# FFN heads of a decoder trunk: weight sums and gate splits put behind the norm, a seven-operation reciprocal root, one raw quarter in the norm's buffer, other tile addresses

## The chip, the cores and the metric

The kernel runs on one core of a Trainium2 chip, in one launch. The metric is the time of an execution on the device in microseconds (us): the median of several runs. The profile and the trace come from one more, profiled execution. Engines are called TensorE (PE in the rows; PEld is its weight load), VectorE (DVE), ScalarE (ACT), GpSimd (POOL) and SyncE (SP, which issues most of the DMAs).

## The reference

The kernel computes a small decoder trunk in fp32 on 512 tokens of 1024 features: two layers of FFN, mixer, FFN. The mixer is a gated convolution in the first layer and sparse attention in the second. Each of the six sub-layers has a norm with a scale, a shift and a gate from a conditioning vector.

```
def adaln(x, g, shift, scale):
    return rms_norm(x, g) * (1 + scale[:, None, :]) + shift[:, None, :]

def swiglu(h, w_in, w_out):
    g, u = jnp.split(h @ w_in, 2, axis=-1)
    return (jax.nn.silu(g) * u) @ w_out
...
        h = adaln(x, norm_g[i, 0], shift[:, 0], scl[:, 0])
        x = x + HALF * gate[:, 0, None, :] * swiglu(h, ffn_w_in[i, 0], ffn_w_out[i, 0])
        h = adaln(x, norm_g[i, 1], shift[:, 1], scl[:, 1])
...
        x = x + gate[:, 1, None, :] * y
        h = adaln(x, norm_g[i, 2], shift[:, 2], scl[:, 2])
        x = x + HALF * gate[:, 2, None, :] * swiglu(h, ffn_w_in[i, 1], ffn_w_out[i, 1])
```

The FFNs are 2816 wide. They are numbered f=0 to 3 here, in the order in which they run.

## The kernel before

`x` lies transposed in SBUF, eight tiles of 128 features by 512 tokens. Every fp32 matrix product is done as three products of fp32r parts (`mm3`, L178 to L180): a value is split into a high part (a copy by ScalarE, L174) and a low part (a subtraction by VectorE, L175), and high by high, low by high and high by low are summed. The names end in `hi`/`lo` or `h`/`l` accordingly. "A group of three" below is one `mm3`.

A sub-layer ends with a tail (`ty`) that works in two halves of 256 tokens, so that the next norm can begin with half 0 while half 1 is still in the tail. The residual (L344) updates `x`, ScalarE squares it (`sq`), and the squares are summed in `nacc` (L243). `Norm.finish` then, for each half, sums over the features on TensorE (`pr`, L260), takes `nv` on VectorE, then the reciprocal root in eleven small operations on 128x2 values (`rs_i` to `rs_r`, L206 to L214), makes two diagonal tiles (`dg`, L267) and spreads them over the partitions with a matmul (`pr`, L268). `piece` makes the normed activation for each of eight feature tiles: `hfull` (L317, VectorE), `hhi` (L319, ScalarE), `hlo` (L320, VectorE). The first matmuls on it are `hs` in `head_start`.

FFNs f=1 to 3 compute most of their columns by a scheme with seven products of half-size blocks in place of eight. Its activation blocks (`th`, `tl`) are made in `quarters`; its weight blocks in `seven_products(j)` come from four raw quarters of a weight tile: two sums of quarters made by DMAs (`qa`), two made by adds (`qb`, L509 and L510), one raw quarter (`a`, named `a22` in the code, L506) and the tile `wraw`. For the first j of each such FFN the two adds run on GpSimd, later on VectorE. `p` (L536) is a copy of the first product that must be made before the accumulator is written again. Ahead of these stands one more pair of columns (`gu`), whose gate weights are `wh` and `wl`.

The engines' queues are in program order, as a scheduler fixed them when the program was built; `tc.high_priority()` moves work forward in them, and `issue_after` (used by the change) keeps an instruction behind another. Tiles live in pools; a tile with a tag takes over the buffer of the tile with that tag before it and waits for its last reader. `tmp` tiles rotate over four buffers of 512 columns. `shift` is a small unused tile that moves everything behind it in the pool to another address.

Of the kernel before, what the change touches and what calls it, by code (L numbers as in the profile page):

```python
# [4 lines left out]

# [17 lines left out]
P = 128  # L23
D = 1024
T = 512
HT = T // 2
KD = D // P
# [26 lines left out]
def decoder_kernel(ctx, tc, xT, cT, ng, adaw, adab, ffi, ffo, cwi, cw, cwo,  # L54
# [8 lines left out]
    def shift(p, n):  # L63
        p.tile([P, n // 4], F32, name="shift")

    shift(pool(ctx, "edge", 1, side="right"), 32)
    cst = pool(ctx, "cst", 1)
    wp = pool(ctx, "wp", 4)
    tp = pool(ctx, "tp", 1)
# [18 lines left out]

    ada_es = ctx.enter_context(ExitStack())
    ap = ada_es.enter_context(tc.tile_pool(name="ada", bufs=4))  # L90
    cond = ap.tile([P, D], F32, name="cond", bufs=1)
    x = [cst.tile([P, T], F32, name=f"x{d}") for d in range(KD)]
    ngs = cst.tile([P, NSUB * KD], F32, name="ngs")
# [107 lines left out]
    def rsqrt(v, n):  # L201
        def small(name, dt=F32):
            return sp.tile([P, n], dt, name=name, padded_shape=[P, 16], bufs=2)

        i = small("rs_i", I32)
        nc.vector.tensor_scalar(i, v.bitcast(I32), 1, None, op0=ALU.logical_shift_right)  # L206
        j = small("rs_j", I32)
        nc.vector.tensor_scalar(j, i, -1.0, RSQ, op0=ALU.mult, op1=ALU.add)
        r = j.bitcast(F32)
        for it in range(3):  # L210
            a, b, q = small("rs_a"), small("rs_b"), small(f"rs_r{it}")
            nc.vector.scalar_tensor_tensor(a, r, -0.5, r, op0=ALU.mult, op1=ALU.mult)
            nc.vector.tensor_mul(b, a, v)
            nc.vector.scalar_tensor_tensor(q, b, 1.5, r, op0=ALU.add, op1=ALU.mult)  # L214
            r = q
        return r

# [8 lines left out]
    class Norm:  # L228
        def __init__(self, s):
            self.s = s  # L230
            self.acc = tp.tile([P, T], F32, name="nacc", tag="nacc", bufs=1)
            self.n = [0, 0]
            self.pr = []

        def square(self, d, a, b, late):
            first = self.n[a // HT] == 0
            if first:
                nc.scalar.activation(self.acc[:, a:b], x[d][:, a:b], AF.Square)
            else:
# [12 lines left out]

        def finish(self, hfs):
            with tc.high_priority():
                n = 2 * len(hfs)
                self.pr += [psum("pr", "pr") for _ in hfs]
                pv = self.pr[hfs[0]]
                for t in range(n):
                    c = hfs[0] * HT + t * P
                    nc.tensor.matmul(pv[:, HT + t:HT + t + 1], self.acc[:, c:c + P], ones[:, 0:1], start=True, stop=True)  # L260
                v = sp.tile([P, n], F32, name="nv", tag="nv", padded_shape=[P, NB])
                nc.vector.tensor_scalar(v, pv[:, HT:HT + n], 1.0 / D, EPS, op0=ALU.mult, op1=ALU.add)
                r = rsqrt(v, n)
                for i, hf in enumerate(hfs):
                    dg = tmp("dg", HT, "dg").rearrange("p (a b) -> p a b", a=2)
                    for t in range(2):
                        nc.vector.tensor_scalar(dg[:, t, :], ident, r[:, 2 * i + t:2 * i + t + 1], None, op0=ALU.mult)  # L267
                    nc.tensor.matmul(self.pr[hf][:, 0:HT], ones, dg.rearrange("p a b -> p (a b)"), start=True, stop=True)  # L268


        def start(self):
            pv = self.all = psum("pr", "pr")
            with tc.high_priority():
                for d in range(KD):
                    dst = self.acc if d == 0 else tmp("sq", tag="sq")
                    nc.scalar.activation(dst, x[d], AF.Square)
                    if d:
                        nc.vector.tensor_tensor(self.acc, self.acc, dst, ALU.add)
                for t in range(NB):
                    nc.tensor.matmul(pv[:, t:t + 1], self.acc[:, t * P:(t + 1) * P], ones[:, 0:1], start=True, stop=True)  # L280
                v = sp.tile([P, NB], F32, name="nv", tag="nv", padded_shape=[P, NB])
                nc.vector.tensor_scalar(v, pv[:, 0:NB], 1.0 / D, EPS, op0=ALU.mult, op1=ALU.add)
                r = rsqrt(v, NB)
                dg = tmp("dg").rearrange("p (a b) -> p a b", a=NB)
                for hf in range(2):
                    for t in range(2 * hf, 2 * hf + 2):
                        nc.vector.tensor_scalar(dg[:, t, :], ident, r[:, t:t + 1], None, op0=ALU.mult)
                    nc.tensor.matmul(self.all[:, hf * HT:(hf + 1) * HT], ones,
                                     dg[:, 2 * hf:2 * hf + 2].rearrange("p a b -> p (a b)"), start=True, stop=True)
# [23 lines left out]
        def piece(self, d, hf):  # L313
            a, b = HALVES[hf]
            sc, sh = mod(self.s, 0, d), mod(self.s, 1, d)
            xr = tmp("xr", HT, "xr") if self.full is None else self.full[:, d, a:b]
            nc.vector.scalar_tensor_tensor(xr, x[d][:, a:b], sc, self.pr[hf][:, 0:HT], op0=ALU.mult, op1=ALU.mult)  # L317
            hi = self.hi[d][:, a:b]
            nc.scalar.activation(hi, xr, AF.Identity, bias=sh)  # L319
            nc.vector.scalar_tensor_tensor(self.lo[d][:, a:b], xr, sh, hi, op0=ALU.add, op1=ALU.subtract)  # L320

        def quarters(self, tt):
            self.th, self.tl = [[tt.tile([P, KD // 2, HT], F32R, name=f"t{e}{j}", tag=f"t{e}{j}") for j in range(4)] for e in "hl"]
# [25 lines left out]

    def head_start(nrm, h, jobs):
        os = [psum("hs") for _ in jobs]
        for hf, (a, b) in enumerate(HALVES):
            with tc.high_priority():
                for d in range(KD):
                    nrm.piece(d, hf)
            m = KD - 3 * hf
            order = [(n, k) for k in range(m) for n in range(len(jobs))]
            order += [(n, k) for n in range(len(jobs)) for k in range(m, KD)]  # L360
            for n, k in order:
                w, wc, kw = jobs[n](k)
                project(os[n][:, a:b], w, wc, h, [(kw, k)], k == 0, k == KD - 1, a, b)
        return os
# [66 lines left out]
    def ffn_first(s, f, nrm, nxt, extra, ahead, first, soon, own):  # L431
        with ExitStack() as es:
            hp = pool(es, "hp", 1)
            hid = Hidden(es, 18)
            h = nrm.alloc(hp)
            nj = FIRST
# [37 lines left out]
    def ffn(s, f, nrm, nxt, w0, ahead):  # L474
        with ExitStack() as es:
# [7 lines left out]
            def seven_products(j):  # L483
# [3 lines left out]
                whi = wp.tile([P, 2, QT], F32R, name="whi", tag="whi", bufs=3)  # L487
                wlo = wp.tile([P, 2, QT], F32R, name="wlo", tag="wlo", bufs=3)
                qa = next(sums)()
                a22 = tmp("a22")  # L490
                qb = swa.tile([P, 2, QT], F32, name="qb")
                ah_, al_ = (sw.tile([P, 2, QT], F32R, name=f"qa{e}", bufs=2) for e in "hl")
                bh_, bl_ = (sw.tile([P, 3, QT], F32R, name=f"qb{e}") for e in "hl")
# [11 lines left out]
                nc.sync.dma_start(raw.rearrange("p a b -> p (a b)"), ffi[f, j, 0].rearrange("p k n -> p (k n)"))  # L505
                nc.sync.dma_start(a22, quart(1, 1))  # L506

                eng = nc.gpsimd if j == nj else nc.vector
                eng.tensor_tensor(qb[:, 0], halves[1], raw[:, 0], ALU.add)  # L509
                eng.tensor_tensor(qb[:, 1], qb[:, 0], raw[:, 1], ALU.add)  # L510
                split(raw, whi, wlo)
                if qa is halves:
                    for n, q in enumerate(qa):
# [35 lines left out]
                keep(e[:, 0:2].rearrange("p a b -> p (a b)"))  # L549

            js = [(j, c) for j in range(nj) for c in range(2)]
            tt = pool(es, "tt", 1, side="right")
            swa = pool(es, "swa", 1, side="right")
            with ExitStack() as tf_es:
                nrm.alloc_seven(hp, pool(tf_es, "tf", 1))
                h = nrm.hi, nrm.lo
                with ExitStack() as hw_es:
                    hw = pool(hw_es, "hw", 1)
                    shift(hw, 64)
                    w = w0 + [weights(ffi[f, j, c], KD, P, hw, 1, wp) for j, c in js[len(w0):]]  # L560

                    gate = weights(ffi[f, nj, 0], KD, P, to=[tt.tile([P, D], F32R, name="w" + e, tag=f"t{e}1") for e in "hl"])
                    os = head_start(nrm, h, [(lambda k, w=w_: (w, 0, k)) for w_ in w])
                os += pair(f, nj, h, gate=gate)
                nrm.quarters(tt)
            nj += 1
# [58 lines left out]
    def conv(s, nrm, nxt, extra, w0, ahead, own):  # L625
        with ExitStack() as es:
            h_es = es.enter_context(ExitStack())
            hp = pool(h_es, "hp", 1)
            ca = pool(es, "cva", 2, side="right")
            h = nrm.alloc(hp)  # L630
            ks = [(k, k) for k in range(KD)]
# [701 lines left out]
```

## Time and profile before

| | |
|---|---|
| median of 3 runs | 1986.33 us (1984.27 to 1987.23) |
| the profiled execution | 1991.76 us, span 1990.0 us |
| TensorE busy | 1935.0 us (97%), 12648 matmuls |
| VectorE busy | 1497.1 us (75%) |
| ScalarE busy | 876.3 us (44%) |
| GpSimd busy | 211.1 us (11%) |
| mean granted TensorE clock | 0.991 of full |
| chain that ended last | TensorE 75%, VectorE 12%, DMA 7%, ScalarE 3% |

The span is the part of the profiled execution that the trace covers. Busy time says how long an engine had an instruction under way; matmuls overlap each other, so the pace of TensorE is read from starts, not from durations. The clock is what was granted to TensorE, as a share of 2.4 GHz.

### The profile page before, as it was taken

The numbers are of one execution on the slowest core, as the hardware profiler recorded it, in microseconds if no ns is written. First come the engines' busy times: TensorE is split into PE (matmuls) and PEld (weight loads), VectorE is DVE, ScalarE is ACT, GpSimd is POOL, SyncE is SP. The second block draws the span as 40 slices with busy tenths as digits, with TensorE's granted clock in tenths as the row PEclk, the third lists the DMA queues.
The fourth block names the chain that finished last, engine by engine and source line by source line (L and its number), as shares of the span: only waits on it lengthen the run. The fifth ranks groups of instructions, "written<-read, shape, count | busy, mean of one in ns | idle before, by whom it ended". The sixth has DMA issues, their size and how long they took to land.

```text
span 1990.0 us, 32476 instructions
## 1 busy us (share of the span) xinstructions
PE 1935.0 (97%) x12648; PEld 1747.0 (88%) x12648; DVE 1497.1 (75%) x2594; ACT 876.3 (44%) x1414; POOL 211.1 (11%) x287
## 2 busy tenths in 40 slices
PE   6999999999999999999999999999989899999999
PEld 4878888898899899999989999999878788898989
DVE  8878888674468686778868677885887878686865
ACT  3422222242235343444534344455777765343532
POOL 0000000100020000001000000001354431000000
PEclk9999999999999999999999999999999899999999
DMA  8888999432246465534646553143211123665622
GB/s 315 293 316 315 325 319 327 161 106 85 85 125 183 132 162 157 149 106 117 181 129 164 153 153 107 45 150 96 54 53 49 60 64 108 184 175 149 170 69 75
DMA packets 113111, 306.88 MB, mean 154 GB/s; under 512 B 13947, under 2 KB 14219, under 8 KB 112956
## 3 DMA queue, kind: packets, MB, share of 16 engines
q1 hardware_dynamic: 97308, 274.81, 41.0%
q0 software_dynamic: 15648, 29.99, 8.8%
q8 instruction: 99, 1.62, 0.3%
q14 instruction: 56, 0.46, 0.1%
HBM read 301.60 MB, written 3.15 MB: 153 GB/s over the span
## 4 chain that ended last, share of the span: by engine, by line
PE 75%; DVE 12%; DMA 7%; ACT 3%; issue 2%; SPq 0%; POOL 0%; DVEq 0%; ACTq 0%; POOLq 0%
PE gu L178 10%; PE gu L180 10%; PE gu L179 10%; PE y L178 6%; PE y L179 6%; PE y L180 6%; DMA adaraw<-in_adaw 6%; DVE wlo L175 3%; PE hs L178 2%; PE hs L179 2%; DVE adaraw L129 2%; PE hs L180 2%; PE cv L179 2%; PE cv L178 2%; PE cv L180 2%
## 5 line engine op out<-in xcount | busy, mean ns | idle before, releaser
L174 ACT ACTIVATE whi<-wraw 128x1024 fp32r<-128x1024 f32 (+2 forms) x283 | 282.0, 1001 | 508.4 <-PE y L179 251.9
L175 DVE TENSOR_TENSOR wlo<-wraw,whi 128x1024 fp32r<-128x1024 f32 (+2 forms) x283 | 326.6, 1155 | 60.5 <-ACT whi L174 58.5
L179 PE MATMUL gu<-hlo,whi 128*128 128x256 f32 (+1 forms) x808 | 258.4, 320 | 0.0
L178 PE MATMUL gu<-hhi,whi 128*128 128x256 f32 (+1 forms) x808 | 258.1, 319 | 0.0
L180 PE MATMUL gu<-hhi,wlo 128*128 128x256 f32 (+1 forms) x808 | 257.4, 319 | 0.0
L178 PE MATMUL y<-ahi,whi 128*128 128x512 f32 x587 | 230.4, 395 | 0.9 <-ACT ahi L174 0.9
L179 PE MATMUL y<-alo,whi 128*128 128x512 f32 x587 | 229.8, 394 | 0.4 <-DVE alo L175 0.4
L180 PE MATMUL y<-ahi,wlo 128*128 128x512 f32 x587 | 229.3, 393 | 0.0
L129 DVE CUSTOM_DVE_ANT_0 adaraw<-adaraw,cond 128x1024 f32<-128x1024 f32 x144 | 174.6, 1224 | 38.5 <-DMA adaraw<-in_adaw 36.8
L178 PEld LDWEIGHTS gu<-hhi,whi 128*128 128x128 f32 x808 | 151.7, 188 | 13.0
L180 PEld LDWEIGHTS gu<-hhi,wlo 128*128 128x128 f32 x808 | 151.7, 188 | 12.3
L179 PEld LDWEIGHTS gu<-hlo,whi 128*128 128x128 f32 x808 | 151.7, 188 | 12.0
L503 POOL DMA_DIRECT2D qa<-in_ffi x54 | 64.9, 1202 | 756.5 <-DMA qa<-in_ffi 289.1
L178 PEld LDWEIGHTS y<-ahi,whi 128*128 128x128 f32 x587 | 109.9, 188 | 29.2 <-ACT ahi L174 5.2
L179 PEld LDWEIGHTS y<-alo,whi 128*128 128x128 f32 x587 | 110.7, 189 | 26.6 <-DVE alo L175 2.9
L180 PEld LDWEIGHTS y<-ahi,wlo 128*128 128x128 f32 x587 | 110.8, 189 | 23.9
L587 DVE SCALAR_TENSOR_TENSOR x<-y,mods,x 128x512 f32<-128x512 f32 x72 | 54.0, 750 | 102.1 <-PE y L180 101.6
L178 PE MATMUL gu<-th,qbh 128*128 128x256 f32 x456 | 126.9, 279 | 2.6 <-ACT qbh L174 2.6
L180 PE MATMUL gu<-th,qbl 128*128 128x256 f32 x456 | 126.5, 279 | 1.8 <-DVE qbl L175 1.8
L178 PE MATMUL gu<-th,qah 128*128 128x256 f32 x456 | 126.1, 277 | 0.6 <-ACT p L536 0.6
L179 PE MATMUL gu<-tl,qbh 128*128 128x256 f32 x456 | 126.7, 278 | 0.0
L179 PE MATMUL gu<-tl,qah 128*128 128x256 f32 x456 | 126.0, 276 | 0.0
(308 smaller groups left out, 5232.4 us busy)
## 6 DMA issues: line engine op xcount, KB each, us to landing
adaraw<-in_adaw SPq DMA_DIRECT2D x144, 512.0 KB, 6.1
wraw<-in_ffi SPq DMA_DIRECT2D x119, 512.0 KB, 3.9
qa<-in_ffi SPq DMA_DIRECT2D x114, 256.0 KB, 3.7
qa<-in_ffi POOLq DMA_DIRECT2D x54, 512.0 KB, 6.4
wraw<-in_ffo SPq DMA_DIRECT2D x72, 384.0 KB, 4.0
a<-in_ffi SPq DMA_DIRECT2D x57, 256.0 KB, 4.2
wraw<-in_cwi SPq DMA_DIRECT2D x24, 512.0 KB, 3.3
wraw<-in_nwi SPq DMA_DIRECT2D x20, 512.0 KB, 3.4
```

The costliest lines, as they stand in the source:

```text
L129: nc.vector.tensor_tensor_reduce(out=raw, in0=raw, in1=cond, scale=1.0, scalar=0.0, op0=ALU.mult, op1=ALU.add, accum_out=m)
L174: nc.scalar.activation(hi, src, AF.Copy)
L175: nc.vector.tensor_tensor(lo, src, hi, ALU.subtract)
L178: nc.tensor.matmul(o, sh, mh, start=first, stop=False)
L179: nc.tensor.matmul(o, sh, ml, start=False, stop=False)
L180: nc.tensor.matmul(o, sl, mh, start=False, stop=last)
L503: nc.gpsimd.dma_start(qa, bass.AP(tensor=a21.tensor, offset=a21.offset, ap=[a21.ap[0], [0, 2], a21.ap[1]]), accum_op=ALU.add)
L587: nc.vector.scalar_tensor_tensor(x[d], o, mod(s, 2, d), x[d], op0=ALU.mult, op1=ALU.add)
```

## The change

- The two weight sums of the first `seven_products` of f=1, 2 and 3 run on VectorE instead of GpSimd, behind the last `hhi`/`hlo` pair of half 1.
- The gate weights' split (`wh`, `wl`) is issued inside `head_start`: behind half 0's last `hhi` on ScalarE and behind half 1's `dg` on VectorE.
- The reciprocal root has ten operations in place of eleven: the first estimate, one Newton step, and one step of higher order (five operations) in place of two more Newton steps.
- The raw quarter `a` of the first `seven_products` takes the buffer of `nacc`, which is now allocated when first used, in place of a `tmp` buffer.
- Unused tiles are added or resized, so that most tiles have other addresses: 96 B in place of 32 at the right edge, 192 B in the pool `ada`, 256 B in `hp` of ffn_first and of conv, 448 B on the right side in `ffn`.

```diff
-    shift(pool(ctx, "edge", 1, side="right"), 32)
+    shift(pool(ctx, "edge", 1, side="right"), 96)
...
+    ap.tile([P, 48], F32, name="shift", bufs=1)
...
-        r = j.bitcast(F32)
-        for it in range(3):
-            a, b, q = small("rs_a"), small("rs_b"), small(f"rs_r{it}")
-            nc.vector.scalar_tensor_tensor(a, r, -0.5, r, op0=ALU.mult, op1=ALU.mult)
-            nc.vector.tensor_mul(b, a, v)
-            nc.vector.scalar_tensor_tensor(q, b, 1.5, r, op0=ALU.add, op1=ALU.mult)
-            r = q
-        return r
+        g = j.bitcast(F32)
+        a, b, r = small("rs_a"), small("rs_b"), small("rs_r0")
+        nc.vector.scalar_tensor_tensor(a, g, -0.5, g, op0=ALU.mult, op1=ALU.mult)
+        nc.vector.tensor_mul(b, a, v)
+        nc.vector.scalar_tensor_tensor(r, b, 1.5, g, op0=ALU.add, op1=ALU.mult)
+
+        a, y, e, p, q = small("rs_a"), small("rs_b"), small("rs_r1"), small("rs_a"), small("rs_r2")
+        nc.vector.tensor_mul(a, r, r)
+        nc.vector.tensor_scalar(e, r, 0.375, None, op0=ALU.mult)
+        nc.vector.tensor_mul(y, a, v)
+        nc.vector.scalar_tensor_tensor(p, y, -10.0 / 3.0, y, op0=ALU.add, op1=ALU.mult)
+        nc.vector.scalar_tensor_tensor(q, p, 5.0, e, op0=ALU.add, op1=ALU.mult)
+        return q
...
+            if d == KD - 1:
+                self.done.append((act, dve))
+        @contextmanager
+        def behind(self, act, dve):
+            with tc.issue_after(act.ins), tc.issue_after(dve.ins):
+                yield
...
-    def head_start(nrm, h, jobs):
+    def head_start(nrm, h, jobs, between=None):
...
+            if hf and between:
+                with nrm.behind(nrm.done[0][0], nrm.diag):
+                    between()
...
-                a22 = tmp("a22")
+                a22 = tp.tile([P, T], F32, name="a22", tag="nacc", bufs=1) if j == nj else tmp("a22")
...
-                eng = nc.gpsimd if j == nj else nc.vector
-                eng.tensor_tensor(qb[:, 0], halves[1], raw[:, 0], ALU.add)
-                eng.tensor_tensor(qb[:, 1], qb[:, 0], raw[:, 1], ALU.add)
+                with nrm.behind(*nrm.done[1]) if j == nj else nullcontext():
+                    nc.vector.tensor_tensor(qb[:, 0], halves[1], raw[:, 0], ALU.add)
+                    nc.vector.tensor_tensor(qb[:, 1], qb[:, 0], raw[:, 1], ALU.add)
...
+            shift(pool(es, "gap", 1, side="right"), 448)
...
-                    gate = weights(ffi[f, nj, 0], KD, P, to=[tt.tile([P, D], F32R, name="w" + e, tag=f"t{e}1") for e in "hl"])
-                    os = head_start(nrm, h, [(lambda k, w=w_: (w, 0, k)) for w_ in w])
+                    to = [tt.tile([P, D], F32R, name="w" + e, tag=f"t{e}1") for e in "hl"]
+                    gate = []
+                    os = head_start(nrm, h, [(lambda k, w=w_: (w, 0, k)) for w_ in w],
+                                    lambda: gate.extend(weights(ffi[f, nj, 0], KD, P, to=to)))
```

The built order shows where this lands. On VectorE in the head of f=3, the end of half 1's reciprocal root and the `dg`, before:

```order
L212 SCALAR_TENSOR_TENSOR rs_a<-rs_r_17193 128x2
L175 TENSOR_TENSOR wl<-wraw,wh 128x1024
L213 TENSOR_TENSOR rs_b<-rs_a,nv 128x2
L214 SCALAR_TENSOR_TENSOR rs_r_17199<-rs_b,rs_r_17193 128x2
L212 SCALAR_TENSOR_TENSOR rs_a<-rs_r_17199 128x2
L213 TENSOR_TENSOR rs_b<-rs_a,nv 128x2
L214 SCALAR_TENSOR_TENSOR rs_r_17205<-rs_b,rs_r_17199 128x2
L267 TENSOR_SCALAR dg<-ident,rs_r_17205 128x128 x2
L317 SCALAR_TENSOR_TENSOR hfull<-x_80,mods,pr 128x256
```

The same place of the changed kernel:

```order
L217 TENSOR_TENSOR rs_a<-rs_r_17172 128x2
L218 TENSOR_SCALAR rs_r_17178<-rs_r_17172 128x2
L219 TENSOR_TENSOR rs_b<-rs_a,nv 128x2
L220 SCALAR_TENSOR_TENSOR rs_a<-rs_b 128x2
L221 SCALAR_TENSOR_TENSOR rs_r_17180<-rs_a,rs_r_17178 128x2
L279 TENSOR_SCALAR dg<-ident,rs_r_17180 128x128 x2
L176 TENSOR_TENSOR wl<-wraw,wh 128x1024
L330 SCALAR_TENSOR_TENSOR hfull<-x_81,mods,pr 128x256
```

`wl` has moved from the middle of the chain to behind the `dg`, ahead of half 1's first `hfull`, and one small operation is gone. On ScalarE in the first `seven_products` of f=3, before (`a_17664` is this product's raw quarter):

```order
L174 ACTIVATE qah<-qa 128x1024
L174 ACTIVATE qbh<-qb 128x1024
L174 ACTIVATE qah<-qa 128x1024
L174 ACTIVATE whi<-wraw 128x1024
L536 ACTIVATE p_17701<-gu 128x256
L174 ACTIVATE ahi<-af 128x512
L174 ACTIVATE whi<-wraw 128x768
L174 ACTIVATE qbh<-a_17664 128x512
```

And in the changed kernel, where the quarter is `a_17645`:

```order
L175 ACTIVATE qah<-qa 128x1024
L175 ACTIVATE qbh<-a_17645 128x512
L175 ACTIVATE qbh<-qb 128x1024
L175 ACTIVATE qah<-qa 128x1024
L175 ACTIVATE whi<-wraw 128x1024
L175 ACTIVATE ahi<-af 128x512
L561 ACTIVATE p_17682<-gu 128x256
```

The quarter's split has moved from the end of this piece to its second place, and `p` now stands behind it and behind `ahi`. On SyncE the quarter's DMA of f=3 stood behind the loads of `wraw` and later quarters, before:

```order
L505 DMA wraw<-in_ffi 128x1024
...
L505 DMA wraw<-in_ffi 128x1024 x2
L189 DMA wraw<-in_ffo 128x768
L496 DMA qa<-in_ffi 128x512 x2
L497 DMA qa<-in_ffi 128x512 x2
L506 DMA a_17664<-in_ffi 128x512
```

Now it stands among the first product's own quarters:

```order
L530 DMA wraw<-in_ffi 128x1024
L521 DMA qa<-in_ffi 128x512
L522 DMA qa<-in_ffi 128x512
L531 DMA a_17645<-in_ffi 128x512
L530 DMA wraw<-in_ffi 128x1024 x2
L190 DMA wraw<-in_ffo 128x768
```

It has moved ahead of the weights and quarters of the products that follow.

## Rows read from the trace of the kernel before

**Rows 1.** Waits of TensorE over the span: waiter, releaser, total us, times, longest.

```profile
PE pr L268 <- DVE dg L267: 3.7, 1, 3.7
...
PE hs L178 <- ACT hhi L319: 3.2, 4, 1.2
...
PE gu L178 <- ACT qbh L174: 2.6, 2, 1.9
PE gu L180 <- DVE qbl L175: 1.8, 1, 1.8
...
PE hs L179 <- DVE hlo L320: 1.0, 1, 1.0
...
PE gu L178 <- ACT p L536: 0.6, 1, 0.6
```

**Rows 2.** Stretches of the heads: length, then busy us of each engine, granted clock.

```profile
590.00:626.00 36.00, 33.61 (x289) 33.08 (x288) 32.65 (x42) 24.84 (x38) 5.87 (x5) 1.00 0.62 143
905.00:936.00 31.00, 28.80 (x211) 27.94 (x210) 25.78 (x77) 13.02 (x27) 4.54 (x4) 0.89 0.55 130
960.00:976.00 16.00, 14.08 (x110) 13.88 (x109) 11.16 (x15) 7.35 (x10) 2.40 (x2) 0.89 0.81 216
1638.00:1660.00 22.00, 17.15 (x131) 16.71 (x130) 20.48 (x50) 11.96 (x26) 4.35 (x4) 0.92 0.30 74
```

**Rows 3.** Timeline of VectorE, head of f=3: start, duration, instruction.

```profile
1642.81 0.16 DVE L262 TENSOR_SCALAR nv<-pr 128x2 f32<-128x2 f32 x1 [0.38 <-PE pr L260]
...
1644.74 2.31 DVE L320 SCALAR_TENSOR_TENSOR hlo<-hfull,mods,hhi 128x256 fp32r<-128x256 f32 x1
1646.98 1.95 DVE L214 SCALAR_TENSOR_TENSOR rs_r<-rs_b,rs_j 128x2 f32<-128x2 f32 x1
...
1649.32 1.21 DVE L175 TENSOR_TENSOR wl<-wraw,wh 128x1024 fp32r<-128x1024 f32 x1
...
1651.42 0.48 DVE L267 TENSOR_SCALAR dg<-ident,rs_r 128x128 f32<-128x128 f32 x2
```

**Rows 4.** Timeline of GpSimd, the same stretch.

```profile
1645.14 1.62 POOL L509 TENSOR_TENSOR qb<-qa,wraw 128x512 f32<-128x512 f32 x1
...
1647.25 1.65 POOL L510 TENSOR_TENSOR qb<-qb,wraw 128x512 f32<-128x512 f32 x1
```

**Rows 5.** Timeline of VectorE, second half of the norm at f=2.

```profile
927.60 0.16 DVE L262 TENSOR_SCALAR nv<-pr 128x2 f32<-128x2 f32 x1 [0.73 <-PE pr L260]
...
933.91 0.49 DVE L267 TENSOR_SCALAR dg<-ident,rs_r 128x128 f32<-128x128 f32 x2
937.75 1.26 DVE L317 SCALAR_TENSOR_TENSOR hfull<-x,mods,pr 128x256 f32<-128x256 f32 x3 [3.35 <-PE pr L268]
```

**Rows 6.** Timeline of ScalarE: the raw quarter at f=2 and f=3.

```profile
969.65 0.63 ACT L174 ACTIVATE qbh<-a 128x512 fp32r<-128x512 f32 x1 [2.63 <-DMA a<-in_ffi]
...
1686.53 0.63 ACT L174 ACTIVATE qbh<-a 128x512 fp32r<-128x512 f32 x1 [1.96 <-DMA a<-in_ffi]
```

**Rows 7.** Timeline of VectorE at f=2: a weight sum of the second product.

```profile
965.53 0.69 DVE L509 TENSOR_TENSOR qb<-qa,wraw 128x512 f32<-128x512 f32 x1
```

**Rows 8.** Timeline of TensorE, ffn_first: every 24th matmul, from one weight tile to another.

```profile
216.03 0.39 PE L178 MATMUL gu<-hhi,whi 128*128 128x512 f32 x1
...
221.47 0.39 PE L178 MATMUL gu<-hhi,whi 128*128 128x512 f32 x1
...
226.97 0.39 PE L178 MATMUL gu<-hhi,whi 128*128 128x512 f32 x1
```

**Rows 9.** Timeline of TensorE at f=2, a stage of `y`: first and 25th matmul.

```profile
1092.21 0.40 PE L178 MATMUL y<-ahi,whi 128*128 128x512 f32 x1
...
1097.81 0.40 PE L178 MATMUL y<-ahi,whi 128*128 128x512 f32 x1
```

**Rows 10.** Timeline of TensorE, tail of ffn_first: first and 19th matmul of 256 columns.

```profile
386.16 0.28 PE L179 MATMUL ty<-alo,whi 128*128 128x256 f32 x1
...
388.32 0.28 PE L179 MATMUL ty<-alo,whi 128*128 128x256 f32 x1
```

More of the change, by code (lines that the diff above doesn't have):

```diff
@@ L1 @@
 import math
-from contextlib import ExitStack, nullcontext
+from contextlib import ExitStack, contextmanager, nullcontext
 from functools import partial
@@ L230, in __init__, with sums @@
             self.s = s
-            self.acc = tp.tile([P, T], F32, name="nacc", tag="nacc", bufs=1)
+            self.acc = None
             self.n = [0, 0]
             self.pr = []
+            self.done = []
+        def sums(self):
+            if self.acc is None:
+                self.acc = tp.tile([P, T], F32, name="nacc", tag="nacc", bufs=1)
         def square(self, d, a, b, late):
+            self.sums()
             first = self.n[a // HT] == 0
@@ L266, in finish @@
                     for t in range(2):
-                        nc.vector.tensor_scalar(dg[:, t, :], ident, r[:, 2 * i + t:2 * i + t + 1], None, op0=ALU.mult)
+                        self.diag = nc.vector.tensor_scalar(dg[:, t, :], ident, r[:, 2 * i + t:2 * i + t + 1], None, op0=ALU.mult)
                     nc.tensor.matmul(self.pr[hf][:, 0:HT], ones, dg.rearrange("p a b -> p (a b)"), start=True, stop=True)
         def start(self):
+            self.sums()
             pv = self.all = psum("pr", "pr")
@@ L318, in piece @@
             hi = self.hi[d][:, a:b]
-            nc.scalar.activation(hi, xr, AF.Identity, bias=sh)
-            nc.vector.scalar_tensor_tensor(self.lo[d][:, a:b], xr, sh, hi, op0=ALU.add, op1=ALU.subtract)
+            act = nc.scalar.activation(hi, xr, AF.Identity, bias=sh)
+            dve = nc.vector.scalar_tensor_tensor(self.lo[d][:, a:b], xr, sh, hi, op0=ALU.add, op1=ALU.subtract)
+            if d == KD - 1:
[4 more added lines that the diff above has]
+                yield
         def quarters(self, tt):
@@ L433, in ffn_first @@
             hp = pool(es, "hp", 1)
+            shift(hp, 256)
             hid = Hidden(es, 18)
@@ L628, in conv @@
             hp = pool(h_es, "hp", 1)
+            shift(hp, 256)
             ca = pool(es, "cva", 2, side="right")
```

## The prediction

> **What bounds the kernel now.** I read the waits of TensorE first, then the stretches around the three FFN heads, then the queues of the engine that each wait names. TensorE is the bound almost everywhere, so only what makes it wait, what lowers its clock or what makes a matmul longer can move the time. Its waits list six lines that belong to the heads of the second, third and fourth FFN (f=1, 2, 3): 3.7 us for a `dg`, 3.2 us for `hhi` (of these four waits, 1.1 us lie in the heads of conv and attention), 2.6 us for `qbh` in two waits, 1.8, 1.0 and 0.6 us [rows 1]. With 0.1 us for another `dg`, seen on TensorE's timeline at f=2, that is 12.9 - 1.1 + 0.1 = 11.9 us. The stretches add what the waits leave behind: the granted clock averages 0.89 over 31 us and over 16 us at f=2, and 0.92 over 22 us at f=3 [rows 2]. With two levels, 2.4 and 1.2 GHz, a mean of 0.89 is 22% of the stretch at the low one, and the work lost is (1 - 0.89) x 31 = 3.4 us, then (1 - 0.89) x 16 = 1.8 and (1 - 0.92) x 22 = 1.8: 7.0 us. Each time the timeline shows the fall just behind a wait. Heads and clock together can give at most 11.9 + 7.0 = 18.9 us.
>
> **The second norm of f=3, step by step.** The chain is on VectorE: `nv`, eleven small operations, two `dg` [rows 3]. It starts at 1642.81 and ends at 1651.42 + 0.48 = 1651.90, and for the last 3.7 us of it TensorE waits [rows 1]. Two of its rows are wrong in size: an `hlo` takes 2.31 us and a 128x2 `rs_r` takes 1.95 us, where the `nv` of the same size takes 0.16 and the `hfull` of `hlo`'s size takes 1.26 / 3 = 0.42 [rows 3, 5]. GpSimd runs its two weight sums at 1645.14 to 1646.76 and 1647.25 to 1648.90 [rows 4], and the two long rows end with them. Moving the sums to VectorE behind the last `hlo` removes both: (2.31 - 0.48) + (1.95 - 0.16) = 3.6 us. `wl` (1.21 us; the next operation starts 0.1 before an operation ends, so 1.1) now stands behind the `dg`: another 1.1. One small operation fewer, 0.16 by the `nv` of its size: 0.2. Together 3.6 + 1.1 + 0.2 = 4.9 us: the `dg` are ready at about 1647.0. TensorE arrived at 1651.9 - 3.7 = 1648.2; it will be there perhaps 0.5 us earlier (the shorter `hhi` wait, one stray gate matmul fewer), at 1647.7. So the wait goes, with some 0.7 us to spare, and I count the whole 3.7. The low clock behind it (1.8 us) goes too: the 1.8 us for `qbl` at f=1, inside the stretch whose clock is 1.00 [rows 1, 2], show that even a wait of that length need not cost any clock, and here nothing is left.
>
> `wl` now delays the first `hfull` of half 1 by up to 1.1 us. Before it, TensorE still has over 3 us of products of half 0 to do behind the second `pr`, so I cost it at nothing; without that cover it would be 1.1 us per head.
>
> The longest wait for `hhi`, 1.2 us at f=3 [rows 1], stands behind `wh` on ScalarE (1.0 us of queue), which now comes after half 0's pieces. The first `hlo` is still behind the last residual's sum on VectorE, so part of the wait only changes its name. Bounds 0 and 1.2; I take 0.5. The shorter `qbh` wait, 2.6 - 1.9 = 0.7 us, follows a DMA [rows 6], treated below. **f=3: 3.7 + 1.8 + 0.5 + 0.7 = 6.7 us.**
>
> **f=2.** Here the first `dg` chain is held up by weight splits and residuals; TensorE then waits 3.2 - 1.1 - 1.2 = 0.9 us for `hhi` and 1.0 for `hlo` [rows 1]. The shorter root and the sums' absence bring the pieces forward by up to 3 us, while TensorE still works on the tail; the first-half `pr` matmul also moves some 33 matmuls forward. I leave 0.3 us for what VectorE can't do in time: 0.1 + 0.9 + 1.0 - 0.3 = 1.7 us. With these waits the 3.4 us of low clock should go. Then TensorE reaches the second `pr` some 5 us earlier, at about 931.7 instead of 937.1. Its `dg` were done at 933.91 + 0.49 = 934.40, 6.8 us behind `nv`, and VectorE afterwards stood idle for 3.35 us [rows 5], so this chain was covered and now nearly isn't. Without `wl` (1.1) and one interleaved step (about 0.5, a small operation and a 128x256 one) it takes 5.2 us, from a `nv` about 1.7 us earlier (the sums of the squares no longer wait for idle TensorE and GpSimd): 927.6 - 1.7 + 5.2 = 931.1. A margin of 0.6 us; if it is missed by a microsecond, that is lost again. **1.7 + 3.4 = 5.1 us.**
>
> **The raw quarter.** `a` is fetched into one of four rotating buffers; its DMA lands at 969.6 and 1686.5, and ScalarE idles 2.63 and 1.96 us for it [rows 6]. From the norm's sum buffer, free as soon as the four column sums are done, the DMA can go out tens of microseconds earlier. What is queued behind it on SyncE are quarters and weights for later products, due over 20 us later. So TensorE's waits for `qbh`, 1.9 and 0.7 us, go, and with the 1.9 the 1.8 us of low clock behind it. At f=1 the quarter had landed, but its low part stood last on VectorE: 1.8 us, which goes as `qbl<-a` now comes right after the first `qal`. In exchange `p` stands behind one more split (0.63 us [rows 6]) and `ahi` of the same shape. f=1 waits for `p` already, 0.6 us [rows 1]; the added cost is between 0 and 1.3 us, and since ScalarE's `qah` there starts on a VectorE that has lost GpSimd's interference, I take 0.4. At f=2 and f=3 `p` had 2 us or more to spare: 0.1. **f=1: 1.8 - 0.4 = 1.4; f=2: 1.9 + 1.8 - 0.1 = 3.6.**
>
> The six sums cost VectorE 2 x 0.69 us a head [rows 7]. They stand ahead of the quarters' differences; at f=2 and f=3 VectorE afterwards waits for ScalarE and the gate products, and at f=1 the lost interference pays for them. Nothing, or 1.4 us per head if VectorE is bound there (rival 2). The shorter root in the other norms: I add nothing.
>
> **The addresses.** No wait, but every matmul is touched. In ffn_first, eight groups of three 512-column matmuls take 221.47 - 216.03 = 5.44 us, the next eight 226.97 - 221.47 = 5.50 [rows 8]: 226.7 and 229.2 ns each, alternating with the pool that the weights lie in. A `y` stage of f=2 runs 24 matmuls in 1097.81 - 1092.21 = 5.60 us [rows 9], 233.3 ns. Pairs of tile addresses explain this: equal remainders in the fast batches, 64 B apart in the slow. Counted over the trace, some 310 groups run at 226.7, 690 at 229, 80 at 233.3. If the new places put all at 226.7, that is 690 x 7 ns + 80 x 20 ns = 6.4 us; nothing, if the pairs are as before; all at 233.3 would cost 310 x 20 + 690 x 13 ns = 15.2 us. The new pairs differ by a multiple of 128 B, nearer to the fast batches, but no row has exactly this pair. I take half of the gain, 3 us.
>
> The Trainium skill, page "SBUF — State Buffer", § "The single rule" and its table, gives the PE two independent read ports and lets only the port pair of VectorE and GpSimd contend. By that rule tile addresses would change no matmul and this term would be 0; rows 8 and 9 show a difference with the place all the same, so I keep the term, halved. The same page's § "SBUF: two separate sides" makes the pair an exclusive lock, which agrees with the 2.31 and 1.95 us of rows 3.
>
> **Sum.** 6.7 + 5.1 + 3.6 + 1.4 = 16.8 at the heads, 3 from addresses: 19.8 us. The profiled execution took 1991.76 us (span 1990.0) and would take 1972.0. The median of the runs is 5.4 us below the profiled one, so I forecast 1986.3 - 19.8 = **1966.5 us**.
>
> **Rivals.**
> 1. *Addresses give nothing* (places don't matter, or fast and slow pairs balance): 16.8 us, 1969.5. For it: no row has the new pair, and some `y` stages with the same remainders differ among themselves.
> 2. *The heads only change their waits.* VectorE, with 1.4 us more per head and `wl` behind the `dg`, is late where TensorE now arrives 5 us earlier (the second `dg` of f=2, `hlo`, `p`): half of 16.8 comes back, with one low-clock stretch. 8 + 2 = 10 us, about 1976. For it: VectorE is busy 20.48 of 22 us at f=3 and 32.65 of 36 at f=1 [rows 2]. Against: of the 20.48, 3.6 us are the two blocked rows.
> 3. *Slow pairs, slower than before.* 512-column groups at 233.3 (+15.2 us) and one in ten of about 2,500 groups of 256 columns at 120 ns, as the tail of ffn_first shows (18 in 388.32 - 386.16 = 2.16 us [rows 10]), against 113 elsewhere: 250 x 20 ns = 5. Then +20.2 - 16.8: 1990. It decides once the matmuls lose more than 16.8 us, 5 ns on each 512-column one.
> 4. *The clock and the waits stay*, the quarter still late because its buffer is held: 1 to 5 us, 1983.
>
> **Chances.** Forecast 0.50 (1961 to 1970), rival 1 0.22 (1967 to 1973), rival 2 0.16 (1972 to 1980), rival 3 0.07, rival 4 0.05. Leaving out 3, 4 and the outer edges, the range is 1960 to 1980. A measurement here can tell about 0.2%, 4 us, from no change. Faster: 0.50 + 0.22 + 0.16 + half of rival 4 = 0.90; within 0.2%: 0.03; slower: 0.07.
>
> **What would show it.** At f=3 no `hlo` or small operation above 0.5 us, no wait for the second `dg`, clock 1.00 in the three stretches. No TensorE wait for `qbh`; a wait for `p` at f=1 near 1 us. `y` and `gu` of 512 columns start 226.7 ns apart. The prediction is wrong if the `dg` of f=2 ends after TensorE arrives, or if these starts lie 229 ns or more apart throughout.

## The result

The changed kernel takes 1958.28 us (median of 4 runs, 1954.91 to 1960.89), the kernel before 1985.3 us in the same comparison: a ratio of 0.9868, 95% interval 0.9841 to 0.9895. A second comparison, at the end of the study, gave 1955.18 against 1985.2 us, 0.9842 (0.9818 to 0.9867). So the change saves 27 to 30 us. The forecast was 19.8 us less, with a range down to 1960.0: the direction was right, the gain too small, and the time lies below the range. One run of e3 below, at 2378 us and a granted clock of 0.753, is left out of its numbers.

The profiled execution took 1954.91 us, its span is 1952.8 us. The page's busy times:

```profile
span 1952.8 us, 32447 instructions
PE 1912.0 (98%) x12648; PEld 1732.9 (89%) x12648; DVE 1485.6 (76%) x2582; ACT 875.1 (45%) x1414; POOL 206.2 (11%) x281
```

Of the waits of TensorE in [rows 1], only these two lines are left in the FFN heads (waiter, releaser, total us, times, longest):

```profile
PE hs L179 <- ACT hhi L332: 0.4, 1, 0.4
...
PE hs L180 <- DVE hlo L333: 0.3, 1, 0.3
```

The stretches of the heads of f=1, f=2, f=3 from the tail's first matmul to the first `y`, with attention as the third line (length, busy TensorE, clock):

```profile
557.30:638.70 81.40, 81.27 (x698) 1.00 0.64 168
890.60:977.80 87.20, 87.15 (x747) 1.00 0.61 161
1229.40:1578.50 349.10, 331.81 (x2423) 0.99 0.24 72
1578.50:1674.60 96.10, 94.82 (x795) 1.00 0.53 138
```

The same stretches of the kernel before, which are longer than those of [rows 2]:

```profile
562.10:646.40 84.30, 81.78 (x697) 1.00 0.61 162
899.00:995.20 96.20, 92.08 (x746) 0.95 0.56 145
1248.70:1607.70 359.00, 338.08 (x2422) 0.97 0.24 70
1607.70:1710.70 103.00, 97.11 (x794) 0.98 0.49 128
```

The heads are 2.9, 9.0 and 6.9 us shorter, 18.8 together. The half-speed stretches at f=2 and f=3 are gone. Attention, which the forecast left alone, is 9.9 us shorter. By these rows TensorE stands idle there for 349.10 - 331.81 = 17.3 us in place of 359.00 - 338.08 = 20.9, which is 3.6 us less; the other 6.3 us are busy time for the same matmuls, at a mean clock of 0.99 in place of 0.97.

VectorE's chain at f=3, to be held against [rows 3]:

```profile
1613.09 0.16 DVE L274 TENSOR_SCALAR nv<-pr 128x2 f32<-128x2 f32 x1 [0.36 <-PE pr L272]
...
1615.43 0.15 DVE L214 SCALAR_TENSOR_TENSOR rs_r<-rs_b,rs_j 128x2 f32<-128x2 f32 x1
1615.50 0.48 DVE L333 SCALAR_TENSOR_TENSOR hlo<-hfull,mods,hhi 128x256 fp32r<-128x256 f32 x1
...
1616.67 0.48 DVE L279 TENSOR_SCALAR dg<-ident,rs_r 128x128 f32<-128x128 f32 x2
1617.07 1.22 DVE L176 TENSOR_TENSOR wl<-wraw,wh 128x1024 fp32r<-128x1024 f32 x1
```

From `nv` to the end of `dg` it takes 4.1 us in place of 9.1; no `hlo` is above 0.48. The wait for this `dg` is off the profile's list. TensorE and the `dg` now arrive together:

```profile
1616.80 0.28 PE L180 MATMUL hs<-hlo,whi 128*128 128x256 f32 x1
1616.91 0.28 PE L181 MATMUL hs<-hhi,wlo 128*128 128x256 f32 x1
1617.21 0.70 PE L280 MATMUL pr<-dg,ones 128*128 128x256 f32 x2
```

The matmul with `dg` starts 0.30 us behind the one before it, where 0.11 us is the pace, and 0.06 us behind the end of the `dg` (1616.67 + 0.48 = 1617.15). So up to 0.2 us may still be waited here.

And the 512-column matmuls, every 24th in ffn_first and then in a `y` stage, to be held against [rows 8, 9]:

```profile
212.18 0.39 PE L179 MATMUL gu<-hhi,whi 128*128 128x512 f32 x1
217.62 0.39 PE L179 MATMUL gu<-hhi,whi 128*128 128x512 f32 x1
223.06 0.39 PE L179 MATMUL gu<-hhi,whi 128*128 128x512 f32 x1
...
1075.16 0.39 PE L179 MATMUL y<-ahi,whi 128*128 128x512 f32 x1
1080.60 0.39 PE L179 MATMUL y<-ahi,whi 128*128 128x512 f32 x1
```

Every step is 5.44 us, 226.7 ns a matmul; the steps of 5.50 and 5.60 are gone.

### The profile page after: what moved, and what is told of

It is laid out like the page before. It is cut to its first block, busy times and chain, and to the rows that moved or that the text cites. A ratio compares the mean times of both kernels' runs of the same rounds, so it can differ in the third digit from the quotient of the medians.

```text
span 1952.8 us, 32447 instructions
## 1 busy us (share of the span) xinstructions
PE 1912.0 (98%) x12648; PEld 1732.9 (89%) x12648; DVE 1485.6 (76%) x2582; ACT 875.1 (45%) x1414; POOL 206.2 (11%) x281
## 4 chain that ended last, share of the span: by engine, by line
PE 77%; DVE 10%; DMA 7%; ACT 3%; issue 2%; SPq 1%; POOL 1%; DVEq 0%; ACTq 0%; POOLq 0%
PE gu L179 11%; PE gu L181 11%; PE gu L180 11%; DMA adaraw<-in_adaw 7%; PE y L179 6%; PE y L180 6%; PE y L181 6%; PE hs L181 2%; PE hs L180 2%; PE hs L179 2%; DVE adaraw L130 2%; DVE wlo L176 2%; PE cv L179 2%; PE cv L181 2%; PE cv L180 2%
## 5 line engine op out<-in xcount | busy, mean ns | idle before, releaser
L181 PE MATMUL gu<-th,qal 128*128 128x256 f32 x456 | 125.9, 276 | 0.0
```

The source lines that it names most:

```text
L181: nc.tensor.matmul(o, sl, mh, start=False, stop=last)
```

## The experiments

Each run has its span and mean granted clock. The clock's part of the time differs between runs of one kernel by up to 20 us, so the table also gives the span times the clock, "at full clock": an estimate of the time if TensorE had always had 2.4 GHz (it also takes out low-clock time in which TensorE waited anyway). The rest is "lost to the clock". Both are means over a kernel's runs; the clock has three digits, which leaves about 1 us for one run. Runs of one kernel scatter by some 2 us at full clock, so a difference of two of these means is known to 1.2 to 2.3 us (95%). The kernel before has 1969.5 to 1969.9 and 13.7 to 17.5 in the comparisons.

| kernel | median us | ratio to before | at full clock | lost |
|---|---|---|---|---|
| changed, first comparison | 1958.3 | 0.9868 | 1947.2 | 8.8 |
| changed again (e12) | 1955.2 | 0.9842 | 1948.6 | 3.9 |
| e1 addresses alone | 1979.5 | 0.9974 | 1965.2 | 14.0 |
| e2 all but addresses | 1961.8 | 0.9879 | 1953.4 | 6.9 |
| e3 sums on GpSimd | 1961.8 | 0.9874 | 1952.4 | 7.5 |
| e4 quarter in a rotating buffer | 1959.0 | 0.9871 | 1952.2 | 6.2 |
| e5 root of eleven | 1963.7 | 0.9877 | 1954.4 | 8.2 |
| e6 gate split early | 1960.0 | 0.9876 | 1949.9 | 10.8 |
| e7 root alone | 1974.2 | 0.9927 | 1964.0 | 8.5 |
| e8 edge of 32 B | 1978.3 | 0.9942 | 1969.0 | 6.3 |
| e9 root in attention | 1982.5 | 0.9978 | 1967.7 | 12.9 |
| e10 root in norms | 1978.5 | 0.9970 | 1965.4 | 12.0 |
| e11 moves alone | 1970.7 | 0.9926 | 1959.4 | 10.2 |

**Addresses alone, and all but addresses.** e1 is the kernel before with these lines; e2 is the changed kernel without them.

```diff
-    shift(pool(ctx, "edge", 1, side="right"), 32)
+    shift(pool(ctx, "edge", 1, side="right"), 96)
+    ap.tile([P, 48], F32, name="shift", bufs=1)
+            shift(hp, 256)      # ffn_first and conv
+            shift(pool(es, "gap", 1, side="right"), 448)
```

> The kernel before with the five unused tiles of the change and nothing else. Theory (addresses were mis-sized: all 512-column groups now start at 226.7 ns apart): 6 us less than before, 0.997, with the head waits as before, and 24 matmuls of every stage of y and gu in 5.44 us. Rival (addresses as forecast or less, the missing 8 us lie in attention): 0 to 3 us less, 0.9985 to 1.000.

> The changed kernel with the unused tiles of the kernel before. Theory (heads 19 us, addresses 6 us): 20 us less than before, 0.990, with no wait for dg, qbh or qbl in the heads and 24 matmuls in 5.44 or 5.50 us as before. Rival (heads 16.8 us, the rest in attention through the shorter root and a moved order): 24 us less or more, 0.988.

At full clock e1 is 1969.5 - 1965.2 = 4.3 us faster than before, and e2 is 5 to 6 us slower than the changed kernel: 4 to 6 us for the addresses, near the theory's 6 and above the 3 of the forecast. In e1 the 512-column matmuls start 227 ns apart throughout, as the theory said. e2 gains 24.8 us by the medians, as the rival said, and 16.1 at full clock. Its heads are what the theory said: 81.2 + 86.6 + 96.3 = 264.1 us, 19.4 less than before, with 0.6 us of waits left at f=3. Attention gains besides, as the rival said: it takes 349.8 us, about as in the changed kernel. So attention's gain isn't the addresses'. In e1 it takes 357.7.

e1 also shows how the head stalls move. It has the order of the kernel before, but here GpSimd's sums of f=1 meet the root and the `dg`, as the timeline shows:

```profile
587.44 2.66 DVE L215 SCALAR_TENSOR_TENSOR rs_r<-rs_b,rs_r 128x2 f32<-128x2 f32 x1
...
588.00 2.08 POOL L511 TENSOR_TENSOR qb<-qa,wraw 128x512 f32<-128x512 f32 x1
```

TensorE waits 4.4 us for that `dg`, where the kernel before had no such wait, and at f=3 the wait of 3.7 us has become 1.6. So the head waits were not as before, which the theory had said of them.

**The parts undone one by one.** e3, e4, e6 and e5 each put one part of the changed kernel back.

```diff
-                with nrm.behind(*nrm.done[1]) if j == nj else nullcontext():   # e3
-                    nc.vector.tensor_tensor(qb[:, 0], halves[1], raw[:, 0], ALU.add)
-                    nc.vector.tensor_tensor(qb[:, 1], qb[:, 0], raw[:, 1], ALU.add)
+                eng = nc.gpsimd if j == nj else nc.vector
+                eng.tensor_tensor(qb[:, 0], halves[1], raw[:, 0], ALU.add)
+                eng.tensor_tensor(qb[:, 1], qb[:, 0], raw[:, 1], ALU.add)
...
-                a22 = tp.tile([P, T], F32, name="a22", tag="nacc", bufs=1) if j == nj else tmp("a22")   # e4
+                a22 = tmp("a22")
```

> The changed kernel with the two weight sums of each head on GpSimd again and not held behind the norm. Theory (the sums block VectorE's operations with two inputs in SBUF): rows of 1.3 to 2.3 us come back among hlo and the root, 3 to 4 us later dg at f=3 and a wait of 2 to 3 us there with a stretch of low clock; 4 to 7 us over the changed kernel. Rival (gate split and root already make enough room): under 1.5 us over it.

e3 is 4 to 5 us slower at full clock. The block came back, but in another place: at f=3 the sums now fall on half 0's chain. The timeline of GpSimd and VectorE there:

```profile
1608.18 1.28 POOL L534 TENSOR_TENSOR qb<-qa,wraw 128x512 f32<-128x512 f32 x1 [7.76 <-DVE rs_r L218]
1608.24 1.23 DVE L220 SCALAR_TENSOR_TENSOR rs_a<-rs_b 128x2 f32<-128x2 f32 x1
...
1609.51 0.16 DVE L221 SCALAR_TENSOR_TENSOR rs_r<-rs_a,rs_r 128x2 f32<-128x2 f32 x1
...
1609.54 1.26 POOL L535 TENSOR_TENSOR qb<-qb,wraw 128x512 f32<-128x512 f32 x1
...
1609.59 1.49 DVE L255 TENSOR_TENSOR nacc<-nacc,sq 128x256 f32<-128x256 f32 x1
```

A 128x2 operation lasts 1.23 us and a 128x256 one 1.49 while a sum runs; free ones take 0.16 and 0.42. TensorE waits 2.1 us for the first `dg` of f=3, where the theory had the second, and 1.2 us for `p` at f=1. A stretch of low clock follows at f=3 (0.98 over its head), as the theory said.

> The changed kernel with the raw quarter a in a rotating buffer again. Theory: the waits for qbh at f=2 and f=3 (1.9 and 0.7 us) and for qbl at f=1 (1.8) come back, with one stretch of low clock: 5 to 6 us over the changed kernel. Rival (the waits came from the late head and are gone with it): under 2 us over it.

e4 is 0.7 us slower by the median of the first comparison, 4 to 5 at full clock. Its waits for `qbh` came back at f=1 and f=3, not at f=2 (total, times, longest):

```profile
PE gu L179 <- ACT qbh L175: 2.4, 2, 1.3
```

So the theory holds at f=3; at f=1 a wait came back for `qbh` in place of `qbl`, at f=2 none, and there was no stretch of low clock in the heads. The waits explain 2.4 us; e4's heads of f=1 and f=3 are 2.0 and 1.9 us longer than those of the changed kernel.

```diff
-                    gate = []
-                    os = head_start(nrm, h, [(lambda k, w=w_: (w, 0, k)) for w_ in w],
-                                    lambda: gate.extend(weights(ffi[f, nj, 0], KD, P, to=to)))
+                    gate = weights(ffi[f, nj, 0], KD, P, to=to)                                    # e6
+                    os = head_start(nrm, h, [(lambda k, w=w_: (w, 0, k)) for w_ in w])
```

> The changed kernel with the gate weights' split issued ahead of the head, as before. Theory (each of the moves clears a part of the chain of half 1): dg at f=3 about 1.2 us later, where 0.7 us were to spare: a wait of about 0.5 us there, hhi at f=3 0.5 us later; 1 to 3 us over the changed kernel. Rival (the sums alone were the chain): no new wait over 0.2 us, 0 to 0.5 us.

e6 is 1 to 3 us slower at full clock, little beyond the scatter. The wait for the second `dg` did not come; the waits for `hhi` and `hlo` at f=3 grew from 0.4 and 0.3 to 1.2 and 0.7 us. The rows of ScalarE, VectorE and TensorE there:

```profile
1608.58 1.06 ACT L175 ACTIVATE wh<-wraw 128x1024 fp32r<-128x1024 f32 x1 [1.04 <-PE ty L181]
...
1610.40 0.74 PE L179 MATMUL hs<-hhi,whi 128*128 128x256 f32 x4 [1.17 <-ACT hhi L332]
...
1610.32 1.22 DVE L176 TENSOR_TENSOR wl<-wraw,wh 128x1024 fp32r<-128x1024 f32 x1
...
1611.99 0.39 PE L180 MATMUL hs<-hlo,whi 128*128 128x256 f32 x1 [0.73 <-DVE hlo L333]
```

So the gate split cost time by standing ahead of half 0's pieces, `wh` ahead of the first `hhi` and `wl` ahead of the first `hlo`, and not by `wl` in the chain of the second `dg`.

> The changed kernel with the root of eleven operations. Theory (attention, 9 us shorter in the changed kernel and not in the addresses-alone kernel, gains by the root that its own norms use, and by the order that the scheduler then finds): attention from its tail matmul to that of the next part about 358 us again, against 349, and 7 to 10 us over the changed kernel. Rival (attention gains by something else, or by its clock alone): attention stays at 349 to 351 us, and under 2 us over the changed kernel.

e5 has the old body of `rsqrt` in the changed kernel. It is 6 to 7 us slower at full clock, a little under the theory's 7 to 10; attention takes 352.7 us, less than the theory's 358 and more than the rival's 351, and a wait of 0.9 us for `hhi` came back at f=2.

**The root by itself.** e7 is the kernel before with the new body of `rsqrt`; e9 and e10 use it in a part of the calls. The new root has ten operations (two for the first estimate, three for the Newton step, five for the last step), not the seven of the title, so it is one shorter than the old.

```diff
-    def rsqrt(v, n):
+    def rsqrt(v, n, short=False):
...
-                r = rsqrt(v, 16)       # attention, queries and keys; rsqrt(v, 1) likewise
+                r = rsqrt(v, 16, True) # e9
...
-                r = rsqrt(v, n)        # the norms; rsqrt(v, NB) likewise
+                r = rsqrt(v, n, True)  # e10
```

> The kernel before with the shorter root and nothing else. Theory (the root brings attention its gain): attention 349 to 352 us, the heads of f=1 to 3 within 2 us of before in sum, 6 to 10 us less than before. Rival (the root is worth one small operation wherever a norm waits): attention 356 us or more, 0 to 2 us less than before.

> The kernel before with the shorter root in attention's own calls (queries, keys) alone; the norms of the six sub-layers keep eleven operations. Theory (the gain that the forecast left out comes where attention normalizes its queries: VectorE's multiply there no longer meets GpSimd's add of x): attention's waits of TensorE 17 us in place of 20.8, no qn of over 2 us, 4 to 6 us less than before once the clock's loss is taken out; heads as before. Rival (it is the sub-layers' norms, or the clock): attention's waits over 19.5 us, under 2 us less.

> The kernel before with the shorter root in the norms of the six sub-layers alone. Theory: attention as before, waits 20 to 21 us; at f=2 and f=3 the waits of the heads fall by 2 to 4 us and the stretch of low clock at f=2 with them, as in the run with the root alone: 2 us less than before without the clock's loss, 5 to 8 us with it. Rival (the root's whole gain is here): attention's waits about 17 us too, the whole 14 us.

e7 was the surprise: one small operation fewer per root, and 14.5 us by the medians, 5.9 us at full clock and 9.0 lost less to the clock. Attention takes 349.1 us. The theory's number for attention is right, but it missed that the heads gain too, 9.5 us in the profiled executions (before's three heads add up to 84.3 + 96.2 + 103.0 = 283.5 us, e7's to 84.0 + 89.9 + 100.1 = 274.0). Of these 9.5 us, 3.6 are idle time of TensorE; the rest is the clock, 1.00 in all three heads of e7. At f=3 one of GpSimd's two sums still meets the second norm's chain, on the `dg`, in place of two on an `hlo` and the root [rows 3, 4]:

```profile
1634.82 2.23 DVE L272 TENSOR_SCALAR dg<-ident,rs_r 128x128 f32<-128x128 f32 x2
...
1635.19 1.57 POOL L515 TENSOR_TENSOR qb<-qb,wraw 128x512 f32<-128x512 f32 x1
```

TensorE waits 1.8 us for it in place of 3.7.

e9 and e10 part it: 2.0 us at full clock in attention, 4.3 in the norms, together about the 5.9 of e7. So my theory for e9, 4 to 6 us, was too high, and that for e10, 2 us, too low; with the clock e10 gains 6.8 us by the medians, within its 5 to 8. TensorE's idle time in attention is 18.4 us in e9, where 17 was expected, and 19.1 in e10, below the 20 to 21: attention, 352.2 us long in e10, seems to gain by the norms too. The mechanism of the theory for e9 shows, though. In e10, with eleven operations in attention, VectorE's multiply of the queries meets GpSimd's add of `x`:

```profile
1464.62 2.84 DVE L772 TENSOR_TENSOR qn<-qn,rs_r 128x512 f32<-128x512 f32 x2
1467.38 0.55 DVE L1079 CUSTOM_DVE_ANT_0 L<-s,tb 128x384 f32<-128x384 f32 x1
...
1465.20 1.71 POOL L1160 TENSOR_TENSOR x<-x,yt 128x512 f32<-128x512 f32 x1
...
1468.20 0.73 PE L1069 MATMUL s<-k,q 128*128 128x512 f32 x2 [1.90 <-DVE st L1079]
```

The operation of L1079, for whose `st` TensorE waits, stands right behind the multiplies. In e9 the same two multiplies are done before that add begins, in 1.28 us, and TensorE's wait of 1.9 us is not there:

```profile
1467.43 1.28 DVE L772 TENSOR_TENSOR qn<-qn,rs_r 128x512 f32<-128x512 f32 x2
...
1470.61 2.53 POOL L1160 TENSOR_TENSOR x<-x,yt 128x512 f32<-128x512 f32 x2
```

In e10 the heads' waits fell by 1.2 us at f=2 and 2.4 at f=3, and the mean clock of the head of f=2 in the profiled execution rose from 0.95 to 1.00.

**The moves alone.** e11 is e2 with the old body of `rsqrt`.

> The changed kernel with the root of eleven operations and the unused tiles of the kernel before: only sums, gate split and raw quarter are moved. Theory (terms add: heads 11 us of waits and 7 of clock; root and addresses apart): heads of f=1 to 3 together 17 to 19 us shorter than before, attention within 3 us of before, 15 to 19 us less than before. Rival (the moves need the shorter root to clear the chains): a wait of 1 us or more is left at f=2 and at f=3 with low clock, 8 to 12 us less.

The heads are 17.6 us shorter (81.3 + 88.3 + 96.3 = 265.9 against 283.5), as the theory said; a wait of 0.9 us for `hhi` at f=2 is left, and attention takes 356.7 us. By the medians e11 gains 14.7 us, just under the theory's 15 to 19; at full clock it gains 10.3. The parts add up: moves 10.3 and root 5.9 (e7) make 16.2, and e2 gains 16.1; with 4 to 6 for the addresses it is 20 to 22, and the changed kernel gains 21.2 to 22.3.

**The edge.** e8 changes one number of the changed kernel.

```diff
-    shift(pool(ctx, "edge", 1, side="right"), 96)
+    shift(pool(ctx, "edge", 1, side="right"), 32)
```

> The changed kernel with 32 B in place of 96 at the right edge: the tiles on that side, among them those of y and ty, lie 64 B further, the instructions and their order are the same. Theory (remainders of moving and weight tiles by 128 B): y starts 229 to 233 ns apart in place of 226.7, 4 to 8 us more in the y stages; the tails' 138 groups of 256 columns at 113 in place of 120 ns, 2.8 us less; gu and cv of 512 columns stay at 226.7. Rival (the gain was that of one pool against another, not of 64 B): no stage changes by over 0.5 us.

e8 is 20 to 22 us slower at full clock, the largest loss of all, with the same order of instructions. `y` does what the theory said, about 229 ns (24 matmuls in 1089.00 - 1083.51 = 5.49 us). But over half of `gu` of 256 columns, which the expectation did not speak of, became slow, 30 matmuls in 3.60 us, 120 ns each:

```profile
1083.51 0.39 PE L179 MATMUL y<-ahi,whi 128*128 128x512 f32 x1
1089.00 0.39 PE L179 MATMUL y<-ahi,whi 128*128 128x512 f32 x1
...
687.61 0.28 PE L179 MATMUL gu<-th,qah 128*128 128x256 f32 x1
...
691.21 0.28 PE L179 MATMUL gu<-th,qbh 128*128 128x256 f32 x1
```

In the changed kernel six of them take 679.88 - 679.20 = 0.68 us, 113 ns:

```profile
679.20 0.28 PE L179 MATMUL gu<-th,qbh 128*128 128x256 f32 x1
...
679.88 0.28 PE L179 MATMUL gu<-th,qbh 128*128 128x256 f32 x1
```

The three stretches between and behind the heads, where these `gu` and the `y` stages lie, are 5.9, 5.8 and 5.4 us longer than in the changed kernel, 17.1 of the loss. The addresses in the built programs tell the two apart: the slow ones have moving and weight tiles with equal remainders by 512 B, the fast ones 64 B away. For 512 columns it is the other way round.

**The changed kernel again.**

> The changed kernel, unaltered. Its time with the clock's loss taken out (span times mean granted clock) was 1947.2 us in four runs, and that of the kernel with the quarter in a rotating buffer 1952.2, while their medians differ by 0.7 us only. If the quarter is worth 5 us and the medians were close by the luck of the clock, this run gives 1946 to 1949 again, with a loss to the clock of 6 to 9 us. If the four runs were lucky, it gives 1950 or more and the quarter is worth little.

It gave 1948.6 us at full clock (1947.1 to 1949.8): the quarter is worth about 4 us, and the near tie of the medians in e4 was the clock's.

None of these kernels beats the changed one, and each part that was taken out of it cost time, the gate split the least.

## Why the prediction was too low

Held against its terms:

- **Second norm of f=3, and the lock.** Right, but not in its margin. `dg` was forecast 4.2 us behind `nv`, and is 4.1. The two long rows, the 3.7 us wait and the low clock behind it are gone. The 0.7 us to spare are not there: TensorE arrives with the `dg`, and that no wait of note is left is in part luck.
- **f=2.** Right in kind; forecast 5.1 + 3.6 = 8.7 us, the head is 9.0 us shorter. The 0.3 us that I left there isn't waited for. The second `dg` is in time, but by 0.15 us and not the forecast's 0.6 (it ends at 922.20 + 0.48 = 922.68, TensorE's matmul starts at 922.83).
- **f=1.** Mis-sized: 1.4 forecast, 2.9 measured. The wait for `p` did not grow to 1 us; it went. ScalarE's queue, which holds one split more, in the changed kernel (first three rows) and before, and behind them the rows of VectorE before that two sums on GpSimd made long:

```profile
607.07 1.06 ACT L175 ACTIVATE qah<-qa 128x1024 fp32r<-128x1024 f32 x1 [0.81 <-DVE tl L176]
608.03 0.61 ACT L175 ACTIVATE qbh<-a 128x512 fp32r<-128x512 f32 x1
...
612.29 0.37 ACT L561 ACTIVATE p<-gu 128x256 f32<-128x256 f32 x1
...
613.97 1.06 ACT L174 ACTIVATE qah<-qa 128x1024 fp32r<-128x1024 f32 x1 [3.10 <-DVE tl L175]
...
617.78 0.36 ACT L536 ACTIVATE p<-gu 128x256 f32<-128x256 f32 x1
...
593.79 3.49 DVE L320 SCALAR_TENSOR_TENSOR hlo<-hfull,mods,hhi 128x256 fp32r<-128x256 f32 x3
```

  With `qah` at 607.07 and `p` at 612.29 the queue between them is 1.4 us longer than before, but measured from the head's start `qah` comes 2.1 us earlier (607.07 - 557.30 = 49.8 against 613.97 - 562.10 = 51.9 us). About 2 us is what VectorE lost to GpSimd before: 3.49 us for three `hlo` of 0.48. I had counted that as 0.9 us at most.
- **The clock.** 7.0 us forecast, and in the heads right: 0.95 over 96.2 us and 0.98 over 103.0 are 4.8 and 2.1 us lost, and all three heads now have 1.00. That a wait of 1.8 us need not cost any clock held again in e10 (1.00 at f=1), but not in e9: with the same wait for `qbl`, and 1.2 us for `p` ahead of it, that head has 0.98. Over the whole kernel the clock's part varies: in the second comparison the loss fell from 13.7 to 3.9 us, 9.8 less; in the first, the 27.0 us of the medians leave 4.7 beside the 1969.5 - 1947.2 = 22.3 at full clock.
- **Addresses.** Right in kind, and the step that halved it was wrong: "no row has exactly this pair. I take half of the gain, 3 us". The 512-column groups run at 226.7 ns; 4 to 6 us were gained. Rival 1 with nothing and rival 3 with slow pairs are both out, though e8 shows that a wrong number costs what rival 3 said, by a way that it did not name: over half of `gu` of 256 columns at 120 ns. The Trainium skill, page "SBUF — State Buffer", § "Who interferes with whom", gives TensorE two independent read ports and names the pair that VectorE and GpSimd share as the only contention. By that, e8 would be as fast as the changed kernel; it is 20 us slower.
- **"The shorter root in the other norms: I add nothing."** This is the step that failed: a term put at nothing without a row for it. Undone, the root costs 6 to 7 us at full clock; added alone it gives 5.9, and more with the clock. I counted one operation of 0.16 us on one chain. What it changes is when VectorE's operations meet GpSimd's: in attention the multiply of the queries no longer stands behind an add (2.84 to 1.28 us, and a wait of 1.9 us of TensorE with it), and in the old head of f=3 one sum in place of two meets the chain. These two are worth 1.9 us of waits each in e7; which meetings the rest comes from is not shown. In the changed kernel the sums are gone from GpSimd: of what e5 loses there, its profile has 3.6 us in attention (352.7 against 349.1) and 1.3 at f=2 (88.5 against 87.2), and where the rest lies is open.
- **Rival 2** (waits only change place) is out: 0.7 us of waits are left in the heads.

The heads, forecast at 16.8 us, gave 18.8. The sum of what was mis-sized, as an estimate: addresses 2 us, f=1 1.5, the root about 5 (5.9 to 7, less what the forecast had of it at f=2 and f=3), and -2 to +3 from the clock; with the forecast's 19.8 that is 26 to 31 us, where 27 to 30 were measured.

Of attention's 9.9 us in the profiled pair, 3.6 are idle time of TensorE and 6.3 the clock, as the stretches under the result show. Open is how much of the clock's part belongs to the change: it differs from one execution to the next (attention takes 349.1 and 350.2 us in two profiles of the changed kernel, 346.4 with a clock of 1.00 in e9), and e5, with the old root, had 0.99 too.

## What to carry to other kernels

Where VectorE and GpSimd both work on SBUF, a short chain is as long as the GpSimd operation that it happens to meet: look for rows of a small form that last far above their mean, and cost a shorter chain by the meetings that it avoids, not by its own operation. Compare variants at the same clock (span times granted clock) when the low-clock time differs from run to run, since medians of a few runs can hide 4 us. And tile addresses are worth a search of their own: 64 B at one edge were worth 20 us here, and the good place for 512 columns is the bad one for 256.

## What the runs showed of the hardware

- Start to start, a matmul of 512 columns takes 226.7 or 229 ns and one of 256 columns 113 or 120 ns, by the addresses of its two tiles: equal remainders by 512 B (or 256 B apart) are fast for 512 columns and slow for 256, and 64 B away from that it is the other way round. Some `y` stages of the kernel before ran at 233 ns with the same remainders as others at 229 [rows 9]; the cause of that is not shown.
- A VectorE operation can be held for a whole GpSimd operation, even on 128x2 values: 1.23 to 2.66 us in place of 0.16.
- With the same order of instructions (before and e1), a shift of the timing by some us turned a wait of 3.7 us at f=3 into one of 1.6, and brought one of 4.4 us at f=1.
